# Seven products in all four pairs of every second MLP step of a two-layer decoder trunk, and a new order of the pairs in the other steps

## The chip, the cores and the metric

The kernel runs on one core of one Trainium2 chip. The metric is the device time of one execution in microseconds (us), the median of several runs; before the change it is 2121.18 us over three runs (2120.37 to 2121.22). TensorE (PE) multiplies matrices, VectorE (DVE) and ScalarE (ACT) work elementwise, POOL and SP issue transfers (DMA); PEld in the profile is TensorE's weight load, which overlaps its matmuls.

## The reference, cut to what matters

Two layers on one sequence of 256 tokens, model width 2048. Layer 0 mixes by a short convolution, layer 1 by stick-breaking attention; each is followed by an MLP with 8192 hidden units, and every part is normalised before and after. Only the MLPs are changed:

```python
def sq_relu_mlp(u, w_up, w_down):
    return jnp.square(jax.nn.relu(u @ w_up)) @ w_down

def reference(x, ...):
    ...
    for i in range(DEPTH):
        ...
        h = h + rmsnorm(m, mix_post_g[i])
        u = rmsnorm(h, mlp_pre_g[i])
        h = h + rmsnorm(sq_relu_mlp(u, mlp_w_up[i], mlp_w_down[i]), mlp_post_g[i])
        ...
```

## The kernel before

Everything is float32. For TensorE each operand is cut into a high part, rounded by ScalarE (whi, hi), and a low part, the rest, taken by VectorE (wlo, lo); one product is three matmuls: high by high, high by low, low by high.

**The steps of an MLP.** The 64 tiles of 128 hidden units are made in STEPS = 8 groups of eight. The first group comes from `lead_up`. Then in each of the steps e = 0 to 6 TensorE alternates eight times between two jobs: `whole_up` makes one hidden tile of the next group (16 matmuls of 512 columns with high parts of the weights, 16 of 256 with low parts, into the one bank UP_BANK), and `Down.pair` multiplies two hidden tiles of the present group by their rows of the down weights. A step has two halves, h = 0 and 1. Each half walks the four pairs m = 0 to 3 for one band of 1024 output columns. I call one up tile with its down pair a place; a step has eight. Step 7 has only down pairs.

**Pairs of eight and of seven.** A pair is a 2x2 by 2x2 product of blocks: two halves of the tokens and two hidden tiles on one side, two hidden tiles and two halves of the band's columns on the other. `eight` does it with eight products, 24 matmuls. `seven` does it with seven (a scheme of Strassen's kind), 21 matmuls, for which sums of blocks are needed on both sides. `split_seven` forms four differences of the weights on VectorE (t1 to t4, line 200, into a buffer with one copy, tag gpre) and cuts seven blocks into parts, in four tiles a, b, t, u of 512, 1024, 1024 and 1024 columns; a pair of eight cuts two weight chunks of 1024. `sums_of` (line 891) forms four sums of the hidden blocks. The table SEVEN says which pairs of a step go by seven: m = 1, 2, 3 in both halves of steps 0 to 6, pair 0 alone in step 7. For a pair of eight the hidden side keeps a difference (`dif`) instead.

**What sets the order.** TensorE's order is that of the code. VectorE's and ScalarE's is fixed when the program is built, by a scheduler that takes the code's order, its priorities and the dependencies. Weights come as chunks of 512 KB from SP, in the order of `step_chunks`, into RAW = 5 buffers; a buffer is loaded again once its chunk is cut. The parts lie in a ring of RING = 7 high and 7 low tiles. `finish` frees the up bank: ScalarE copies one half of it (`half`, line 927), VectorE adds the other (`s`, line 861), and the next up tile can begin.

**The end of a down projection.** An object `Down` collects one band over eight pairs: the second half of a step and the first half of the next. At its last pair VectorE adds three banks into the results (line 968), ScalarE copies four others out (line 983), and POOL adds these into the results by transfers (line 931, three with each of the next up tiles). So it always ends with the fourth place of a step, and the fifth follows, a pair of eight here.

Of the kernel before, what the change touches and what calls it, by code (L numbers as in the profile page):

```python
# [9 lines left out]
F32 = mybir.dt.float32  # L10
F32R = mybir.dt.float32r
# [3 lines left out]
P = 128  # L15
# [31 lines left out]
STEPS = 8  # L47
NF = FF // STEPS // P
UP_BANK = 2
DOWN_BANKS = {(0, 0): 3, (0, 1): 4, (1, 0): 5, (1, 1): UP_BANK, 1: 6, 5: 7, 6: 0, 7: 1}  # L50
LAST_BANKS = [[6, 7], [0, 1]]
SEVEN = [((1, 2, 3), (1, 2, 3))] * 7 + [((0,), ())]

IN_N = [j * KD + i for i in range(KD) for j in range(3)]

# [11 lines left out]
def band_of(e, h):  # L67

    return 1 - (h + e) % 2


def step_chunks(e):

    return [
        (kind, c)
        for h in range(2) for m in range(4)
        for kind, c in [("up", 8 * h + 2 * m + t) for t in range(2)]
        + [("dn", band_of(e, h) * 8 + 2 * m + t) for t in range(2)]
    ]

# [6 lines left out]
def trunk(ctx, tc, x, xT, vecs, rows, ws, out):  # L87
# [149 lines left out]
    def operand(name):  # L237
        return act.tile([P, 4, 2, NB, P], F32R, tag="x4", name=name)
# [119 lines left out]
    def inverse_root(total, bias, scale=1.0 / D):  # L358
        r = small("rstd")
        nc.scalar.activation(r[:], total, AF.Sqrt, bias=bias, scale=scale)  # L360
        nc.vector.reciprocal(r[:], r[:])
        return r

    class Norms:
# [119 lines left out]
        def input(self, b, c):  # L484

            self.u[b, c] = piece(h[b], c)
            if self.gpre is not None:
                t = self.u[b, c] = self.pool.tile([P, 6 * P], F32, tag="hg", name="hg", bufs=4)[:, :512]
                with tc.high_priority():
                    nc.vector.tensor_tensor(t, piece(h[b], c), piece(self.gpre, c), op=ALU.mult)  # L490

# [121 lines left out]
    class OutNorms(Norms):  # L613
# [6 lines left out]
            self.order.__enter__()  # L620

        def post(self, b, c, src, to, scale=None):
            t = self.pool.tile([P, 6 * P], F32, tag="hg", name="mgg", bufs=4)[:, :512] if c > 1 else to
            nc.scalar.activation(
                self.dump()[:], src, AF.Square, scale=1.0 if scale is None else scale,
                accum_out=self.ss[b][:, c : c + 1],
            )
            self.gained(b, c, src, t, scale)
            if (b, c) == (1, 2):
                self.residual(0, 3, [0])  # L630
            if c == 2:
                self.add_up(b)
            elif c == 3:
                self.r[b] = inverse_root(self.ss[b][:, 3:4], self.bias[b][:])
                for i in range(3):
# [198 lines left out]
    def mlp(pool, i, before, after):  # L834
# [5 lines left out]
        def two_parts(parts, src):  # L840
            hi, lo = parts
            nc.scalar.activation(hi, src, AF.Copy)
            nc.vector.tensor_tensor(lo, src, hi.bitcast(F32), op=ALU.subtract)

        class Hidden:


            def __init__(self, e):
                self.xs, self.sums = [None] * (NF // 4), {}
                first, second = SEVEN[e]  # L850
                self.pairs = [2 * m for m in first]
# [6 lines left out]
            def tile(self, n, ps, half):  # L858
                s = pool.tile([P, T], F32, tag="s", name="s", bufs=3)
                with tc.high_priority():  # L860
                    nc.vector.tensor_tensor(s[:], ps[:, :T], half[:], op=ALU.add)  # L861
                nc.scalar.activation(s[:], s[:], AF.Relu)  # L862
                nc.scalar.activation(s[:], s[:], AF.Square)
                if self.xs[n // 4] is None:
                    self.xs[n // 4] = operand("hid4")
                if n in self.pairs and n not in self.apart:
                    two_parts(self.x(n, 0), s[:, :P])
                else:
                    split_tile(self.xs, n, s[:])
                if n in self.pairs:  # L870
                    held[n] = s
                elif n - 1 in self.pairs:
                    self.sums[n - 1] = self.sums_of(n - 1, held.pop(n - 1), s)
                elif n - n % 2 in self.eights:
                    if n % 2 == 0:
                        self.sums[n] = pool.tile([P, 2, 2, P], F32R, tag="d", name="sums", bufs=2)
                    parts = [self.sums[n - n % 2][:, n % 2, j, :] for j in range(2)]
                    d = pool.tile([P, P], F32, tag="dif", name="dif", bufs=1)
                    nc.vector.tensor_tensor(d[:], s[:, :P], s[:, P:], op=ALU.subtract)
                    two_parts(parts, d[:])  # L880

            def sums_of(self, n, x, y):

                t = after.dump()
                s1, s2, s3, s4 = (t[:, j * P : (j + 1) * P] for j in range(4))
                a11, a21, a12, a22 = x[:, :P], x[:, P:], y[:, :P], y[:, P:]
                for to, v, w, op in (
                    (s1, a21, a22, ALU.add), (s2, s1, a11, ALU.subtract),
                    (s3, a11, a21, ALU.subtract), (s4, a12, s2, ALU.subtract),
                ):  # L890
                    nc.vector.tensor_tensor(to, v, w, op=op)
                if n in self.apart:
                    one = pool.tile([P, 2 * P], F32R, tag="s1", name="sums", bufs=1)
                    one = [one[:, j * P : (j + 1) * P] for j in range(2)]
                else:
                    one = self.x(n, 1)
                more = pool.tile([P, 6 * P], F32R, tag="hg", name="sums", bufs=4)
                more = [more[:, j * 3 * P : (j + 1) * 3 * P] for j in range(2)]
                two_parts(one, s1)
                two_parts(more, t[:, P:])  # L900
                return [one] + [[m[:, j * P : (j + 1) * P] for m in more] for j in range(3)]
# [99 lines left out]
        class Down:  # L1001


            def __init__(self, j, plan):
                self.j, self.plan, self.ps = j, plan, {}
                sevens_at = [at for at in plan if at[1] in SEVEN[at[0]][at[2]]]
                whole_at = [at for at in plan if at not in sevens_at and at[0] == STEPS - 1]
# [17 lines left out]
            def pair(self, at, first, xs):  # L1025
                e, m, _ = at
                seven = m in SEVEN[e][at[2]]
                (self.seven if seven else self.eight)(at, first, xs, 2 * m)
# [42 lines left out]
        for e in range(STEPS):  # L1071
            for h in range(2):
                for m in SEVEN[e][h]:
                    n = 16 * h + 4 * m + 2 if e < STEPS - 1 else 8 * h + 2 * m
                    sevens[W["mlp", i, e + 1].base + n] = pool
        now = Hidden(0)
        lead_up(now)
        for e in range(STEPS):
            first = W["mlp", i, e + 1].base
            if e == STEPS - 1:  # L1080
                for b in range(NB):
                    scale[b] = small("hs")
                    nc.vector.tensor_tensor(scale[b][:], before.hs[b][:], before.hs[b][:], op=ALU.mult)
                after.gpost = row(pool, (B_MPOST0, B_MPOST1)[i], "gpost")
                turned["banks"] = [2, 3]
                for m in range(4):
                    down.pair((e, m, 0), first + 2 * m, now)
                run(
                    [Group(first + 8, 8, now.xs, LAST_BANKS, lambda b, c, ps: add(band_of(e, 1), b, c, ps, True))],
                    leave=after,  # L1090
                )
                break
            new = Hidden(e + 1)
            for h in range(2):
                if e == 0 or h == 1:
                    plan = [(e, m, h) for m in range(4)]
                    if h == 1:
                        plan += [(e + 1, m, 0) for m in range(4)]
                    down = Down(band_of(e, h), plan)
                for m in range(4):  # L1100
                    at_chunk = first + 16 * h + 4 * m
                    whole_up(new, 4 * h + m, at_chunk, UP_BANK)
                    down.pair((e, m, h), at_chunk + 2, now)
            now = new

# [180 lines left out]
    for j in range(4):  # L1286
        for i, (name, to, scale) in enumerate((
            ("k", kT, lambda b: kv.hs[b][:]), ("q", qT, lambda b: held["rq", b][:]),
        )):
            n = 2 * j + i  # L1290
# [86 lines left out]
```

## Time and profile before

| | |
|---|---|
| median of three runs | 2121.18 us (2120.37 to 2121.22) |
| profiled execution | 2121.52 us, its span 2119.8 us |
| matmuls on TensorE | 10816 |
| VectorE, ScalarE instructions | 2557, 2136 |
| TensorE's granted clock, mean | 0.999 of full |
| DMA packets | 449.24 MB in all, mean 212 GB/s |

The span runs from the first to the last instruction; the profiled execution's own time is 1.7 us longer. The first MLP takes about 380 to 1021 us of the span, the second about 1450 to its end. A row of a timeline has the start (us), the duration (us), engine, line, operation, the tiles written and read, shapes and a count; a bracket tells how long the engine stood idle before and for whom. Durations on TensorE and VectorE overlap a little with the next instruction, so the distance of two starts is the better price of an instruction in a row of many.

### The profile page before, as it was taken

What the parts mean: (1) busy time and instruction counts of PE and PEld (TensorE: products, weight loads), DVE (VectorE), ACT (ScalarE), POOL (GpSimd) and SP (SyncE); (2) the same over time, 40 slices, a digit from 0 to 9 for tenths busy, and PEclk for the clock granted to TensorE, in tenths of its full rate; (3) what the DMA queues carried; (4) which work ended last, traced back from release to release, by engine and by line L of the source; (5) the groups of instructions that cost most, each with busy time, mean ns of one, the idle gap of its engine ahead of it and who ended that gap; (6) DMA issues with size and microseconds to landing.
All of it is one profiled execution on the core that took longest, in us unless ns stands there. A gap on an engine that the chain in (4) does not pass through costs nothing.

```text
span 2119.8 us, 29868 instructions
## 1 busy us (share of the span) xinstructions
PE 2109.0 (99%) x10816; PEld 1805.5 (85%) x10816; DVE 1700.5 (80%) x2557; ACT 1389.6 (66%) x2136; POOL 112.6 (5%) x135
## 2 busy tenths in 40 slices
PE   9999999999999999999999999999999999999998
PEld 8888888888888888888888888889888888888886
DVE  7766655889889888989866777558898889898987
ACT  7554444777766766766567888547767667676664
POOL 0000000010110100101000000000101001011010
PEclk9999999999999999999999999999999999999999
DMA  8655564676877867869575545655678688687693
GB/s 314 214 188 189 189 238 140 206 224 216 253 210 221 249 205 237 243 202 272 163 229 173 159 159 159 218 179 183 201 223 237 209 238 245 203 255 220 210 265 138
DMA packets 132341, 449.24 MB, mean 212 GB/s; under 512 B 14816, under 2 KB 15072, under 8 KB 131168
## 3 DMA queue, kind: packets, MB, share of 16 engines
q1 hardware_dynamic: 113472, 408.65, 58.7%
q0 software_dynamic: 18432, 38.28, 9.2%
q8 instruction: 85, 1.39, 0.3%
q14 instruction: 64, 0.52, 0.1%
q10 hardware_dynamic: 288, 0.39, 0.1%
HBM read 413.19 MB, written 2.10 MB: 196 GB/s over the span
## 4 chain that ended last, share of the span: by engine, by line
PE 99%; DMA 0%; DVE 0%; ACT 0%; SPq 0%; issue 0%; DVEq 0%; ACTq 0%
PE up L914 21%; PE up L921 12%; PE acc L719 11%; PE acc L300 8%; PE acc L302 8%; PE acc L301 7%; PE acc L1021 5%; PE acc L1022 5%; PE acc L1023 5%; PE more L1022 4%; PE more L1021 4%; PE more L1023 4%; PE lead L719 1%; PE up L916 1%; PE tr L253 1%; DMA raw<-w_in 0%
## 5 line engine op out<-in xcount | busy, mean ns | idle before, releaser
L174 DVE TENSOR_TENSOR wlo<-raw,whi 128x1024 fp32r<-128x1024 f32 (+1 forms) x506 | 605.2, 1208 | 201.3 <-ACT whi L163 129.9
L163 ACT ACTIVATE whi<-raw 128x1024 fp32r<-128x1024 f32 (+1 forms) x506 | 525.7, 1046 | 232.3 <-PE acc L302 84.0
L914 PE MATMUL up<-u,whi 128*128 128x512 f32 x1952 | 465.0, 389 | 0.0
L914 PEld LDWEIGHTS up<-u,whi 128*128 128x128 f32 x1952 | 365.0, 188 | 74.7
L921 PEld LDWEIGHTS up<-u,wlo 128*128 128x128 f32 x2048 | 263.6, 191 | 10.3
L921 PE MATMUL up<-u,wlo 128*128 128x256 f32 x2048 | 268.0, 283 | 0.0
L931 POOL DMA_DIRECT2D mg<-more x108 | 100.3, 977 | 1292.1 <-ACT s L862 582.7
L176 DVE SCALAR_TENSOR_TENSOR wlo<-raw,gv,whi 128x512 fp32r<-128x512 f32 (+1 forms) x160 | 131.8, 853 | 41.5 <-ACT whi L163 40.8
L719 PE MATMUL acc<-u,whi 128*128 128x512 f32 x672 | 156.5, 390 | 0.0
L300 PE MATMUL acc<-whi,u 128*128 128x512 f32 x384 | 153.1, 399 | 0.1
L163 ACT ACTIVATE whi<-raw,gv 128x512 fp32r<-128x512 f32 (+1 forms) x160 | 121.6, 800 | 48.2 <-PE acc L302 42.0
L302 PE MATMUL acc<-whi,u 128*128 128x512 f32 x384 | 149.9, 390 | 0.0
L301 PE MATMUL acc<-wlo,u 128*128 128x512 f32 x384 | 149.7, 390 | 0.0
L719 PEld LDWEIGHTS acc<-u,whi 128*128 128x128 f32 x672 | 124.8, 188 | 25.0
L927 ACT ACTIVATE half<-up 128x256 f32<-128x256 f32 x128 | 48.7, 383 | 113.6 <-PE up L921 112.0
L200 DVE TENSOR_TENSOR sums<-raw,sums 128x512 f32<-128x512 f32 x172 | 117.8, 685 | 1.5
L302 PEld LDWEIGHTS acc<-whi,u 128*128 128x128 f32 x384 | 72.1, 188 | 15.3
L719 PEld LDWEIGHTS acc<-u,wlo 128*128 128x128 f32 x672 | 83.5, 192 | 1.7
L719 PE MATMUL acc<-u,wlo 128*128 128x256 f32 x672 | 84.2, 283 | 0.0
L300 PEld LDWEIGHTS acc<-whi,u 128*128 128x128 f32 x384 | 72.2, 188 | 13.9 <-ACT tk L1214 0.6
L301 PEld LDWEIGHTS acc<-wlo,u 128*128 128x128 f32 x384 | 72.3, 188 | 13.4
L862 ACT ACTIVATE s<-s 128x256 f32<-128x256 f32 x128 | 52.1, 410 | 33.5 <-DVE s L861 32.4
(4476 smaller groups left out, 4065.5 us busy)
## 6 DMA issues: line engine op xcount, KB each, us to landing
raw<-w_mlp SPq DMA_DIRECT2D x512, 512.0 KB, 4.7
raw<-w_in SPq DMA_DIRECT2D x94, 512.0 KB, 4.2
mg<-more POOLq DMA_DIRECT2D x108, 256.0 KB, 8.0
raw<-w_out SPq DMA_DIRECT2D x32, 512.0 KB, 3.6
raw<-w_v SPq DMA_DIRECT2D x32, 512.0 KB, 4.4
raw<-w_k SPq DMA_DIRECT2D x32, 512.0 KB, 4.0
raw<-w_q SPq DMA_DIRECT2D x32, 512.0 KB, 3.7
raw<-w_wo SPq DMA_DIRECT2D x32, 512.0 KB, 3.7
```

The lines of the kernel that those rows point to most:

```text
L163: rounded = nc.scalar.activation(hi[:, at], raw[i][:, at], AF.Copy, scale=1.0 if gain is None else gain)
L174: nc.vector.tensor_tensor(lo[:, at], t[:, at], hi[:, at].bitcast(F32), op=ALU.subtract)
L176: nc.vector.scalar_tensor_tensor(lo[:, at], t[:, at], gain, hi[:, at].bitcast(F32), op0=ALU.mult, op1=ALU.subtract)
L300: nc.tensor.matmul(ps[:], xh, hi[:, a], start=i == 0 and k == 0, stop=False)
L301: nc.tensor.matmul(ps[:], xh, lo[:, a], start=False, stop=False)
L302: nc.tensor.matmul(ps[:], xl, hi[:, a], start=False, stop=i == self.n - 1 and k == self.ks - 1)
L719: nc.tensor.matmul(ps[:, :cols], w, xs[:, :cols], start=k == 0 and part == parts[0], stop=k == KD - 1 and part == parts[1], skip_group_che ...
L914: nc.tensor.matmul(ps, weight(0, first, m), x, start=k == 0, stop=False)
L921: nc.tensor.matmul(pss[n][:, :T], weight(1, first, m), x, start=False, stop=k == KD - 1)
L1021: nc.tensor.matmul(self.ps[key][:], xh, hi, start=first, stop=False)
L1022: nc.tensor.matmul(self.ps[key][:], xh, lo, start=False, stop=False)
L1023: nc.tensor.matmul(self.ps[key][:], xl, hi, start=False, stop=last)
```

## The change

In steps 0, 2, 4 and 6 all four pairs go by seven products in both halves. In steps 1, 3 and 5 pair 0 still goes by eight; the first half walks the pairs 0, 1, 2, 3 as before, the second 1, 2, 3, 0, so that the pair of eight stands first and last in the step. The second half of every step uses that order, in the stored weights too. Step 7 is as it was. The buffers of the sums become one of a larger form (tag d, which now also serves `one` in step 7), and the tag hg has five copies in place of four.

```diff
-SEVEN = [((1, 2, 3), (1, 2, 3))] * 7 + [((0,), ())]
+SEVEN = [((0, 1, 2, 3),) * 2 if e % 2 == 0 else ((1, 2, 3),) * 2 for e in range(STEPS - 1)] + [((0,), ())]
+ORDER = ((0, 1, 2, 3), (1, 2, 3, 0))
...
-        for h in range(2) for m in range(4)
-        for kind, c in [("up", 8 * h + 2 * m + t) for t in range(2)]
+        for h in range(2) for i, m in enumerate(ORDER[h])
+        for kind, c in [("up", 8 * h + 2 * i + t) for t in range(2)]
         + [("dn", band_of(e, h) * 8 + 2 * m + t) for t in range(2)]
...
-                t = self.u[b, c] = self.pool.tile([P, 6 * P], F32, tag="hg", name="hg", bufs=4)[:, :512]
+                t = self.u[b, c] = self.pool.tile([P, 6 * P], F32, tag="hg", name="hg", bufs=5)[:, :512]
...
-                        self.sums[n] = pool.tile([P, 2, 2, P], F32R, tag="d", name="sums", bufs=2)
+                        self.sums[n] = pool.tile([P, 2, 2, P], F32R, tag="d", name="sums", bufs=1)
...
-                    one = pool.tile([P, 2 * P], F32R, tag="s1", name="sums", bufs=1)
-                    one = [one[:, j * P : (j + 1) * P] for j in range(2)]
+                    one = pool.tile([P, 2, 2, P], F32R, tag="d", name="sums", bufs=1)
+                    one = [one[:, 0, j, :] for j in range(2)]
...
-                more = pool.tile([P, 6 * P], F32R, tag="hg", name="sums", bufs=4)
+                more = pool.tile([P, 6 * P], F32R, tag="hg", name="sums", bufs=5)
...
-                    n = 16 * h + 4 * m + 2 if e < STEPS - 1 else 8 * h + 2 * m
+                    n = 16 * h + 4 * ORDER[h].index(m) + 2 if e < STEPS - 1 else 8 * h + 2 * m
...
-                    plan = [(e, m, h) for m in range(4)]
+                    plan = [(e, m, h) for m in ORDER[h]]
                     if h == 1:
-                        plan += [(e + 1, m, 0) for m in range(4)]
+                        plan += [(e + 1, m, 0) for m in ORDER[0]]
                     down = Down(band_of(e, h), plan)
-                for m in range(4):
-                    at_chunk = first + 16 * h + 4 * m
-                    whole_up(new, 4 * h + m, at_chunk, UP_BANK)
+                for n, m in enumerate(ORDER[h]):
+                    at_chunk = first + 16 * h + 4 * n
+                    whole_up(new, 4 * h + n, at_chunk, UP_BANK)
                     down.pair((e, m, h), at_chunk + 2, now)
```

How the instructions move is shown at the fifth place of step 4 of the first MLP, just behind the end of a down projection. A line number in the changed kernel is one higher. First TensorE, before: the last half of a pair of eight, each factor of it an ordinary weight chunk (a product is here two times three matmuls, one for each chunk).

```order
L1021 MATMUL acc<-whi_7790,sums 128x512
L1022 MATMUL acc<-wlo_7791,sums 128x512
L1023 MATMUL acc<-whi_7790,sums 128x512
L1021 MATMUL acc<-whi_7826,sums 128x512
L1022 MATMUL acc<-wlo_7827,sums 128x512
L1023 MATMUL acc<-whi_7826,sums 128x512
L1021 MATMUL more<-whi_7790,hid_6631 128x512
L1022 MATMUL more<-wlo_7791,hid_6631 128x512
L1023 MATMUL more<-whi_7790,hid_6631 128x512
L1021 MATMUL more<-whi_7826,hid_6631 128x512
L1022 MATMUL more<-wlo_7827,hid_6631 128x512
L1023 MATMUL more<-whi_7826,hid_6631 128x512
```

After: the last part of the pair of seven in its place, with t and u, the differences of the weights (290 is the pair's first chunk).

```order
L1022 MATMUL more<-whi290t,hid_6673 128x512
L1023 MATMUL more<-wlo290t,hid_6673 128x512
L1024 MATMUL more<-whi290t,hid_6673 128x512
L1022 MATMUL more<-whi290t,sums 128x512
L1023 MATMUL more<-wlo290t,sums 128x512
L1024 MATMUL more<-whi290t,sums 128x512
L1022 MATMUL more<-whi290u,sums 128x512
L1023 MATMUL more<-wlo290u,sums 128x512
L1024 MATMUL more<-whi290u,sums 128x512
L1022 MATMUL acc<-whi290u,hid_6673 128x512
L1023 MATMUL acc<-wlo290u,hid_6673 128x512
L1024 MATMUL acc<-whi290u,hid_6673 128x512
```

The pair has 21 matmuls now in place of 24, three for each of seven products. Next VectorE at the same place, before: the low part of the pair's first chunk, then s of the fourth place's up tile, two of the three additions of the finished down projection (line 968), the pair's second chunk, the chunks of the next up tile (wlo_7833, wlo_7847) and work on hidden sums (sq, hid).

```order
L174 TENSOR_TENSOR wlo_7791<-raw_7702,whi_7790 128x1024
L861 TENSOR_TENSOR s<-up,half 128x256
L968 TENSOR_TENSOR mg<-mg,acc 128x512 x2
L174 TENSOR_TENSOR wlo_7827<-raw_7704,whi_7826 128x1024
L891 TENSOR_TENSOR sq<-s 128x128
L174 TENSOR_TENSOR wlo_7833<-raw_7732,whi_7832 128x1024
L968 TENSOR_TENSOR mg<-mg,acc 128x512
L248 TENSOR_TENSOR hid_7468<-s,hid_7468 128x256
L891 TENSOR_TENSOR sq<-sq,s 128x128
L843 TENSOR_TENSOR hid_7468<-sq,hid_7468 128x128
L891 TENSOR_TENSOR sq<-s,sq 128x128
L174 TENSOR_TENSOR wlo_7847<-raw_7746,whi_7846 128x1024
```

After: s stands behind the low parts of the fifth up tile's second chunk and of the pair's a; the parts b and t of the pair lie between the additions (line 969 now).

```order
L175 TENSOR_TENSOR wlo_7796<-raw_7700,whi_7795 128x1024
L175 TENSOR_TENSOR wlo290a<-raw_7755,whi290a 128x512
L862 TENSOR_TENSOR s<-up,half 128x256
L969 TENSOR_TENSOR mg<-mg,acc 128x512
L175 TENSOR_TENSOR wlo290b<-raw_7757,whi290b 128x1024
L969 TENSOR_TENSOR mg<-mg,acc 128x512
L892 TENSOR_TENSOR sq<-s 128x128
L175 TENSOR_TENSOR wlo290t<-sums,whi290t 128x1024
L969 TENSOR_TENSOR mg<-mg,acc 128x512
L249 TENSOR_TENSOR hid_7524<-s,hid_7524 128x256
L892 TENSOR_TENSOR sq<-sq,s 128x128
L844 TENSOR_TENSOR hid_7524<-sq,hid_7524 128x128
```

Ahead of s VectorE now has the four differences of the fifth pair, and behind it the low parts of b, t and u, with u after the rows shown; before, two chunks of 1024 were all of that pair's work.

More of the change, by code (lines that the diff above doesn't have):

```diff
@@ L622, in post @@
         def post(self, b, c, src, to, scale=None):
-            t = self.pool.tile([P, 6 * P], F32, tag="hg", name="mgg", bufs=4)[:, :512] if c > 1 else to
+            t = self.pool.tile([P, 6 * P], F32, tag="hg", name="mgg", bufs=5)[:, :512] if c > 1 else to
             nc.scalar.activation(
```

## The prediction

> **What bounds the kernel now.** I read the page first, then TensorE's waits, then windows of one MLP step.
>
> ```profile
> span 2119.8 us, 29868 instructions
> PE 2109.0 (99%) x10816; PEld 1805.5 (85%) x10816; DVE 1700.5 (80%) x2557; ACT 1389.6 (66%) x2136; POOL 112.6 (5%) x135
> ...
> PE 99%; DMA 0%; DVE 0%; ACT 0%; SPq 0%; issue 0%; DVEq 0%; ACTq 0%
> ```
>
> ```profile
> PE warm L709 <- DVE ones L104: 1.1, 1, 1.1
> PE lead L719 <- ACT whi L163: 0.7, 1, 0.7
> PE tr L253 <- DVE h L480: 0.3, 1, 0.3
> ```
>
> The chain is TensorE alone, and these are all the waits it has (us, times, longest): 2.1 us. VectorE's 80% is an average over stages, so I take the MLP apart. The next rows are windows (length, then busy time of PE, PEld, DVE, ACT, POOL, the granted clock, DMA share, GB/s): eight pairs of an MLP, then one pair of eight products and one of seven, each from the first matmul of its up tile to that of the next.
>
> ```profile
> 787.00:871.00 84.00, 84.00 (x431) 72.05 (x431) 74.70 (x111) 57.91 (x89) 7.94 (x10) 1.00 0.77 229
> ```
>
> ```profile
> 788.64:799.65 11.01, 11.01 (x57) 9.43 (x56) 10.06 (x18) 6.85 (x14) 4.42 (x5) 1.00 1.05 265
> 799.65:809.98 10.33, 10.33 (x55) 8.86 (x53) 9.54 (x13) 7.51 (x11) 2.61 (x3) 1.00 1.08 284
> ...
> 851.96:862.29 10.33, 10.33 (x54) 8.86 (x53) 10.05 (x16) 7.33 (x12) 0.00 (x0) 1.00 0.69 213
> ```
>
> TensorE has no hole at the full clock. A pair of eight takes 11.01 us, one of seven 10.33; two of eight and six of seven make 2 x 11.01 + 6 x 10.33 = 84.0 us, the window. VectorE works 74.7 of these 84.0 us: it is second, 9.3 us behind, and what the change gives it to do decides the case.
>
> **What is removed.** The order of TensorE has 48 matmuls of 128x512 less: in steps 0, 2, 4 and 6 of both MLPs two pairs go from eight products in 24 matmuls to seven in 21, so 4 x 2 x 2 = 16 pairs by 3. Their pace, from rows whose first matmuls start 16 apart:
>
> ```profile
> 851.96 3.79 PE L914 MATMUL up<-u,whi 128*128 128x512 f32 x16
> 855.59 2.08 PE L921 MATMUL up<-u,wlo 128*128 128x256 f32 x16
> ```
>
> (855.59 - 851.96) / 16 = 0.227 us, so 48 x 0.227 = **10.9 us**; the two kinds of pair say the same, 16 x (11.01 - 10.33) = 10.9. Their weight loads go with them. SP issues as many loads as before, since the new place of pair 0 in the second half is changed in the stored weights and in the stream alike, and POOL as many additions. The Trainium skill (TensorE: Matmul & The Clock Gate, section Back-to-back issue gap) gives about 131 ns per matmul of 512 columns in a sustained stream; by that the term would be 6.3 us and the profiled execution 2115.2. This case's trace disagrees, with 227 ns over every such stretch, and the measurement stands.
>
> **What is added.** Each of the 16 pairs now costs VectorE four differences of weights (t1 to t4), and low parts for 3584 columns (a of 512, b, t, u of 1024) in place of 2048.
>
> ```profile
> 802.54 0.68 DVE L200 TENSOR_TENSOR sums<-raw 128x512 f32<-128x512 f32 x1
> 803.14 0.68 DVE L200 TENSOR_TENSOR sums<-raw,raw 128x512 f32<-128x512 f32 x1
> ...
> 862.23 1.23 DVE L174 TENSOR_TENSOR wlo318u<-sums,whi318u 128x1024 fp32r<-128x1024 f32 x1
> 863.37 0.28 DVE L843 TENSOR_TENSOR hid<-s,hid 128x128 fp32r<-128x128 f32 x1
> ```
>
> Back to back a 512-wide operation takes 0.60 us (803.14 - 802.54), a 1024-wide one 1.14 (863.37 - 862.23). So 4 x 0.60 + 1.14 + 0.60 = 4.14 us more per pair, 8.3 us per step of all sevens. ScalarE's high parts grow likewise by a 1024-wide and a 512-wide one:
>
> ```profile
> L163 ACT ACTIVATE whi<-raw 128x1024 fp32r<-128x1024 f32 x498 | 523.0, 1057 | 230.9 <-PE acc L302 84.0 <-PE up L914 67.6 <-PE acc L719 38.3
> L163 ACT ACTIVATE whi<-raw,gv 128x512 fp32r<-128x512 f32 x128 | 85.4, 714 | 35.4 <-PE acc L302 34.0 <-issue 1.4
> ```
>
> about 1.06 + 0.71 = 1.8 us a pair, 57.9 + 3.5 = 61.4 us of a step of 82.6: hidden under TensorE with 21 us to spare; without that cover it would cost 8 x 3.5 = 28. The sums of the hidden tiles change little: where an eight's pair becomes a seven's, two differences of 128x128 with their splits and a 128x256 split give way to four 128x128 sums, a 128x384 and two 128x128 and one 128x256 split, which at the same rows' pace is 0.5 us, and falls in the step before, an odd one with room. The merged sums buffer and the fifth hg buffer add no instruction; a tile of the next step is made after the last product that reads the old one, so I cost them at nothing, covered by TensorE (about 1 us of wait a step, at most 14, if a release came late).
>
> **Does VectorE fit?** A step of all sevens takes TensorE 84.0 - 2 x 0.68 = 82.6 us and VectorE 74.7 + 8.3 = 83.0: 0.4 over. An odd step takes 84.0 and 75.2. So in half the steps VectorE is full, and its waits decide. In the quoted window they are:
>
> ```profile
> DVE wlo310u L174 <- ACT whi310u L208: 2.5, 1, 2.5
> DVE wlo L174 <- PE up L921: 2.3, 1, 2.3
> DVE wlo L174 <- issue: 2.0, 1, 2.0
> DVE wlo294u L174 <- ACT whi294u L208: 1.6, 1, 1.6
> ```
>
> ```profile
> ACT whi294u L208 <- PE more L1023: 2.4, 1, 2.4
> ...
> ACT whi310u L208 <- PE more L1023: 1.8, 1, 1.8
> ```
>
> The two on ScalarE go back to TensorE: the ring of seven parts was full, VectorE was as far ahead as it may be. Such waits vanish once it is late; they are slack, not demand. How late may it be? Two deadlines: the up bank (one bank, freed by s, then taken by the next up tile), and the last parts of the weights.
>
> ```profile
> 815.72 0.38 ACT L927 ACTIVATE half<-up 128x256 f32<-128x256 f32 x1 [1.28 <-PE up L921]
> 816.58 0.42 DVE L861 TENSOR_TENSOR s<-up,half 128x256 f32<-128x256 f32 x1
> 820.30 3.79 PE L914 MATMUL up<-u,whi 128*128 128x512 f32 x16
> ...
> 871.26 0.39 PE L1021 MATMUL more<-whi318u,sums 128*128 128x512 f32 x1
> ```
>
> s ends at 817.00 and the bank is wanted at 820.30: 3.3 us. wlo318u ends at 863.46 and is used from 871.26: 7.8 us. In the run of sevens s follows half at once (0.5 us), so the lag is not growing there today. With 0.4 us too much per step and 3.3 us to hold it until the next pair of eight gives back 4.1, VectorE should just fit. The order keeps s ahead of the next pair's b, t and u parts; behind it wait, in the fifth pair, the three additions of the finished down projection, which a pair of eight used to cover.
>
> A second full place is the first pair of each MLP, right behind the lead-up, which becomes one of seven:
>
> ```profile
> 409.00:451.00 42.00, 42.00 (x224) 36.31 (x224) 39.05 (x71) 31.92 (x61) 0.00 (x0) 1.00 0.54 173
> ```
>
> 39.05 + 4.14 + 0.5 = 43.7 us of VectorE in 42.0 - 0.7 = 41.3: 2.4 over, held for a time by the same two deadlines.
>
> For all this TensorE's stall has no row of before. Below it is nothing (all of the lag held by the bank; it can't be a gain, since TensorE has no wait to lose). Above, if all 9.3 us of idle time stayed, a step would take 83.0 + 9.3 = 92.3 in place of 82.6, 78 us over the 8 steps. Nearest to it are the excesses that the rows give: 8 x 0.4 for the full steps and 2 x 2.4 for the lead-ups, 8.0 us. Each of them alone is under the 3.3 us of the bank and could vanish; I take a fifth for the places where two meet, **1.5 us**.
>
> **Sum.** 2121.52 (the profiled execution: span 2119.8 and 1.7 around it) - 10.9 + 1.5 = 2112.1. The median of the runs, 2121.18, is 0.3 lower, so **2111.8 us**, 9.4 or 0.44% faster. Below about 0.2% (4.2 us) a measurement of this kernel tells nothing.
>
> **Rival 1, VectorE takes over (slower).** Its order is fixed, and in a full step each wait that isn't TensorE's doing comes back as a hole of TensorE. For it: 83.0 against 82.6, and the runs of up to nine sevens in a row where there were three. Against: the waits above are TensorE's. It decides when more than about 1.0 us a step (a step then exceeds 84.0) is lost for good. With half of the idle time kept, a step takes 83.0 + 4.65 = 87.7, 3.7 over 84.0: 8 x 3.7 = 29 us over today, **2151**.
>
> **Rival 2, the loads pace it (no change).** When a down projection ends, POOL's additions into the results crowd the queues:
>
> ```profile
> raw<-w_mlp SPq DMA_DIRECT2D x512, 512.0 KB, 4.7
> ```
>
> ```profile
> L147 SPq DMA_DIRECT2D raw<-w_mlp x9: 327/328/328, 788.2 to 808.4; - x9
> ...
> DMA to landing us min/median/max: 5.4/7.4/8.4
> ```
>
> ```profile
> DVE sums L200 <- DMA raw<-w_mlp: 3.7, 4, 1.7
> ```
>
> The first row is the median over all loads (4.7 us), the next that stretch (7.4), the last VectorE's waits at 451 to 475, where such additions begin in step 0. A seven holds both raw buffers until its differences are done, so loads start late when time is short. For it: the DMA share of 1.05 and 1.08 in the pairs above, now under a seven too. Against: at 787 to 871 VectorE waits for no load. If each of the 14 ends cost 3.7 us, less the 3.3 of the bank but with the 0.5 by which s lags already, 14 x 0.9 = 12.6 us would be lost: 2121.2 - 10.9 + 12.6 = **2122.9**.
>
> **Rival 3, it doesn't do what it says.** The saved matmuls could be missing, at 2121.2. The order shows them gone and nothing else new on TensorE.
>
> **Chances.** The forecast 0.66; rival 1 0.16; rival 2 0.16; rival 3 0.02. The forecast's case runs from no stall, 2121.2 - 10.9 = 2110.3, to four times the stall, 2116. Rival 2 scatters to both sides of 2121, a quarter of it still below 2116.9. The range **2109.5 to 2124** holds the forecast, most of rival 2 and rival 3; its low end is no stall less the 0.8 between the runs. Rival 1 is left out but for its foot, since the price between nothing and 78 us has no upper row near. Faster by over 0.2%: 0.66 + 0.04 = 0.70; within: 0.10; slower: 0.20.
>
> **What would show it.** Eight pairs of an even step in 82.6 us with PE busy throughout and no row of TensorE waiting for s or for wlo; VectorE near 82 of these, its ring waits gone; odd steps at 84.0. Wrong it is if TensorE waits for s (the bank) or wlo in the fifth to eighth pair of even steps (rival 1), or VectorE's t1 and t3 wait for raw with holes of TensorE right behind, at the ends of the down projections (rival 2).

## The result, and the profile after

| | before | after |
|---|---|---|
| median, the same chip (us) | 2121.2 (2120.37 to 2121.41) | 2112.5 (2111.68 to 2113.6) |
| ratio, 95% interval | | 0.996 (0.9947 to 0.9973) |
| profiled execution, its span (us) | 2121.52, 2119.8 | 2111.68, 2110.0 |

The change makes the kernel 8.7 us faster; forecast were 9.4 us and 2111.8. The profiled execution is the fastest of the six runs after the change, so its profile may show less of what is lost than a median run would.

First the page of the changed kernel: its head, the busy time of each engine (us, share, instructions), and the chain of work that ended last.

```profile
span 2110.0 us, 29980 instructions
...
PE 2098.2 (99%) x10768; PEld 1795.9 (85%) x10768; DVE 1766.0 (84%) x2669; ACT 1409.4 (67%) x2168; POOL 112.6 (5%) x135
...
PE 96%; DVE 1%; DMA 1%; ACT 0%; issue 0%; SPq 0%; DVEq 0%; ACTq 0%
```

TensorE has 48 matmuls less and its busy time fell by 2109.0 - 2098.2 = 10.8 us. Its idle time grew from 2119.8 - 2109.0 = 10.8 to 2110.0 - 2098.2 = 11.8 us. The chain, which was TensorE alone, now leaves it for VectorE and a transfer for 1% each. VectorE's busy time grew by 65.5 us and ScalarE's by 19.8; POOL's is the same.

TensorE's waits in the changed kernel (us in total, times, longest) name the place where the chain leaves it:

```profile
PE up L915 <- DVE s L862: 1.3, 2, 0.8
PE warm L710 <- DVE ones L105: 1.1, 1, 1.1
PE lead L720 <- ACT whi L164: 0.4, 2, 0.2
```

The first row is new: twice an up tile waits for s, which frees its bank. To find where, here are windows of the first MLP, one per step from 0 to 4 (length, then busy time of PE, PEld, DVE, ACT, POOL, the granted clock, DMA share, GB/s):

```profile
409.84:492.50 82.66, 82.66 (x426) 70.93 (x425) 80.19 (x125) 63.03 (x105) 7.05 (x8) 1.00 0.72 212
492.50:576.50 84.00, 83.16 (x427) 71.02 (x426) 76.45 (x114) 58.72 (x93) 7.01 (x8) 1.00 0.77 236
...
577.61:660.20 82.59, 82.59 (x425) 70.90 (x424) 79.86 (x117) 61.07 (x93) 7.91 (x9) 1.00 0.75 224
660.20:744.20 84.00, 84.00 (x431) 72.02 (x430) 78.70 (x122) 58.26 (x92) 7.92 (x9) 1.00 0.76 240
744.20:826.80 82.60, 82.60 (x425) 70.90 (x424) 79.63 (x112) 60.83 (x91) 7.92 (x9) 1.00 0.73 221
```

Every even step takes 82.6 us with TensorE busy throughout. Only the window of step 1 has a hole (83.16 of 84.00 busy; the window is one of 84 us laid over the step, so it doesn't hold all of a step that has grown). Inside step 1, the fifth, sixth and seventh place in the same columns:

```profile
534.49:544.82 10.33, 10.33 (x54) 8.86 (x53) 10.30 (x18) 10.33 (x19) 5.27 (x6) 1.00 0.90 182
544.82:556.15 11.33, 10.49 (x55) 8.68 (x53) 7.26 (x11) 4.58 (x8) 1.74 (x2) 1.00 1.06 300
555.83:566.30 10.47, 10.15 (x52) 8.73 (x53) 10.47 (x17) 7.94 (x13) 0.00 (x0) 1.00 0.70 231
```

All three are places with a pair of seven and should take 10.33 us. The sixth takes 11.33 and the seventh 10.47. In the second MLP the same two places of step 1 take 10.91 and 10.47. Together 1.00 + 0.14 + 0.58 + 0.14 = 1.9 us are lost there, and no other place of a step is longer than its 10.33 or 11.01. In the sixth place VectorE is busy for only 7.26 of 11.33 us: it isn't short of time there, it waits. Its timeline in the first MLP (start, duration, operation, and in brackets how long it stood idle before and for whom):

```profile
549.94 0.69 DVE L201 TENSOR_TENSOR sums<-raw 128x512 f32<-128x512 f32 x1 [1.37 <-DMA raw<-w_mlp]
553.33 0.69 DVE L201 TENSOR_TENSOR sums<-raw,raw 128x512 f32<-128x512 f32 x1 [2.70 <-DMA raw<-w_mlp]
553.94 1.22 DVE L175 TENSOR_TENSOR wlo<-raw,whi 128x1024 fp32r<-128x1024 f32 x1
555.07 0.69 DVE L201 TENSOR_TENSOR sums<-raw,sums 128x512 f32<-128x512 f32 x1
555.68 0.42 DVE L862 TENSOR_TENSOR s<-up,half 128x256 f32<-128x256 f32 x1
```

and on ScalarE and TensorE what s belongs to:

```profile
550.56 0.38 ACT L928 ACTIVATE half<-up 128x256 f32<-128x256 f32 x1
```

```profile
548.45 2.08 PE L922 MATMUL up<-u,wlo 128*128 128x256 f32 x16
...
556.15 3.93 PE L915 MATMUL up<-u,whi 128*128 128x512 f32 x16 [0.84 <-DVE s L862]
```

ScalarE's half is done at 550.94, and s could start. VectorE starts it at 555.68, because its fixed order has three differences and a low part ahead of s, and two of the differences wait for chunks that haven't landed (1.37 and 2.70 us). s ends at 556.10, and TensorE's next up tile starts at 556.15, 0.84 us after the engine ran dry. The loads behind it, by SP's queue from 535 to 557, with the time from issue to landing:

```profile
L148 SPq DMA_DIRECT2D raw<-w_mlp x6: 327/328/1351, 541.6 to 555.2; - x6
...
DMA to landing us min/median/max: 4.8/8.3/11.5
```

In that window the first load is issued at 541.6, and a load takes 8.3 us at the median and up to 11.5, against 4.7 over all loads of the kernel before. Two things meet at 535 to 545. First, a buffer comes free late. ScalarE is busy for all 10.33 us of the fifth place, VectorE for 10.30. ScalarE copies results of the finished down projection (L984) beside its usual work, and the high parts for the sixth up tile stand behind the copies; VectorE takes the first low part after that, and the load follows its end:

```profile
537.88 1.09 ACT L984 ACTIVATE more<-more 128x512 f32<-128x512 f32 x2
538.83 2.04 ACT L164 ACTIVATE whi<-raw 128x1024 fp32r<-128x1024 f32 x2
```

```profile
540.34 1.22 DVE L175 TENSOR_TENSOR wlo<-raw,whi 128x1024 fp32r<-128x1024 f32 x1
```

Second, POOL's additions run (5.27 and 1.74 us of POOL in the two places) while the late loads are under way. That is a reading of the rows; the experiments test it.

The fourteen ends of down projections in the steps 0 to 6 (seven in each MLP) differ in how long VectorE waits for loads behind them. In windows of some 25 us it waits 4.1 us behind the end above, and behind that of step 1 in the second MLP (from 1602 to 1628)

```profile
DVE sums L201 <- DMA raw<-w_mlp: 3.7, 2, 2.2
```

These are the two ends that lose, and both waits are longer than the 3.3 us that the prediction read as the up bank's room. Behind the other twelve VectorE waits 0 to 2.6 us, and TensorE loses nothing.

### The profile page after: what moved, and what is told of

Same layout as the page of the kernel before. It is cut to its first block, busy times and chain, and to the rows that moved or that the text cites. A ratio compares the mean times of both kernels' runs of the same rounds, so it can differ in the third digit from the quotient of the medians.

```text
span 2110.0 us, 29980 instructions
## 1 busy us (share of the span) xinstructions
PE 2098.2 (99%) x10768; PEld 1795.9 (85%) x10768; DVE 1766.0 (84%) x2669; ACT 1409.4 (67%) x2168; POOL 112.6 (5%) x135
## 4 chain that ended last, share of the span: by engine, by line
PE 96%; DVE 1%; DMA 1%; ACT 0%; issue 0%; SPq 0%; DVEq 0%; ACTq 0%
PE up L915 20%; PE up L922 11%; PE acc L720 11%; PE acc L301 8%; PE acc L303 8%; PE acc L302 8%; PE more L1023 5%; PE more L1022 5%; PE more L1024 5%; PE acc L1022 4%; PE acc L1023 4%; PE acc L1024 4%; PE lead L720 1%; PE up L917 1%; DMA raw<-w_mlp 1%; PE tr L254 1%
## 5 line engine op out<-in xcount | busy, mean ns | idle before, releaser
L175 DVE TENSOR_TENSOR wlo<-raw,whi 128x1024 fp32r<-128x1024 f32 (+1 forms) x474 | 566.5, 1206 | 149.4 <-ACT whi L164 123.7
L164 ACT ACTIVATE whi<-raw 128x1024 fp32r<-128x1024 f32 (+1 forms) x474 | 489.7, 1045 | 206.5 <-PE acc L303 84.0
L201 DVE TENSOR_TENSOR sums<-raw,sums 128x512 f32<-128x512 f32 x204 | 139.5, 684 | 1.3
```

The costliest lines, as they stand in the source:

```text
L164: rounded = nc.scalar.activation(hi[:, at], raw[i][:, at], AF.Copy, scale=1.0 if gain is None else gain)
L175: nc.vector.tensor_tensor(lo[:, at], t[:, at], hi[:, at].bitcast(F32), op=ALU.subtract)
L201: nc.vector.tensor_tensor(t, x, y, op=ALU.subtract)
```

## The experiments

The kernel before took 2121.0 to 2121.2 us on the chips of these runs. Each time is a median with its range, each ratio is to the kernel before.

**1. The old order of pairs.** The even steps keep their sevens; in the second half of a step the pairs go 0, 1, 2, 3 again, so the fifth place of an odd step is a pair of eight.

```diff
-ORDER = ((0, 1, 2, 3), (1, 2, 3, 0))
+ORDER = ((0, 1, 2, 3), (0, 1, 2, 3))
```

> The changed kernel with the order 0, 1, 2, 3 in both halves, as before the change: in odd steps the pair of eight stands first and fifth again. My theory: the whole 10.9 us come from the 48 matmuls, and what is lost (2.2 us of the median) is lost where a load comes late behind the end of a down projection in step 1, with a pair of seven in the fifth place. With the pair of eight back there the loss of step 1 goes: 2110.3 to 2111.3, and TensorE doesn't wait for s in step 1. Rival (the new order is what lets the sevens fit): VectorE falls behind without it, 2114 or more, with TensorE waiting for s or for wlo in several steps.

Measured: 2110.18 us (2110.07 to 2111.34), ratio 0.9951 (0.9938 to 0.9963); none of its runs is as slow as the fastest of the change. No row of TensorE waiting for s is left. The sixth place of step 1 in windows, and SP's loads from 535 to 557:

```profile
545.40:555.73 10.33, 10.33 (x54) 8.86 (x53) 7.78 (x10) 5.99 (x9) 0.98 (x2) 1.00 1.02 279
```

```profile
L148 SPq DMA_DIRECT2D raw<-w_mlp x8: 328/328/1244, 539.7 to 556.2; - x8
...
DMA to landing us min/median/max: 3.7/7.2/10.7
```

The place is whole again, and the time is the expected one to 0.1 us. The loads still land late (7.2 us), but the first is issued 1.9 us earlier. It follows the low part of the sixth up tile's first chunk, as in the change; VectorE starts that part at 538.40 here and at 540.34 there, ScalarE the high part ahead of it at 536.97 and at 538.83. With a pair of eight in the fifth place both engines have less to do ahead of it. So with the old order the sevens of the even steps gain 10.8 us, and the new order gives 2.3 of it back. (The profile has small losses yet: the seventh and eighth places of step 0 are up to 0.2 us longer than they should be.)

**2. The new order alone.** SEVEN as before the change; order and buffers as in the change.

```diff
-SEVEN = [((0, 1, 2, 3),) * 2 if e % 2 == 0 else ((1, 2, 3),) * 2 for e in range(STEPS - 1)] + [((0,), ())]
+SEVEN = [((1, 2, 3),) * 2 for e in range(STEPS - 1)] + [((0,), ())]
```

> The new order alone: pair 0 goes by eight products in all steps 0 to 6 as before the change, but stands last in each second half. My theory: no matmul goes, so nothing is won, and the fifth place is now a seven behind each end of a down projection: 2121.2 to 2122.5, with at most a stall for s in step 1. Rival (part of the gain is the order's): under 2119.

Measured: 2124.28 us (2123.07 to 2125.4), ratio 1.0015 (1.0006 to 1.0024): 3.3 us slower than before, more than expected. TensorE's waits of this kernel:

```profile
PE up L915 <- DVE s L862: 1.4, 4, 0.4
```

The holes lie in the sixth and seventh places of steps 0 and 1 in both MLPs, with a little in step 2 of the first. The same wait appears with no added product of seven anywhere, behind the same ends, where a pair of seven now stands in the fifth place.

The order is not all that is new here, though. The diff leaves one copy of the buffer for an eight's sums (tag d) where there were two, and of the same form. The changed kernel has pairs of eight in every second step only, and one copy is enough. Here every step has them, and the old sums are read until the eighth place. So the second difference (`dif`) of the first two hidden tiles that step 0 makes, done at 432.04 in the kernel before, is done at 497.74 in this one:

```profile
432.04 0.28 DVE L879 TENSOR_TENSOR dif<-s 128x128 f32<-128x128 f32 x1
```

```profile
497.74 0.28 DVE L880 TENSOR_TENSOR dif<-s 128x128 f32<-128x128 f32 x1
```

One of the three copies of s is held all that time. Steps 3 to 6 hold it as long and have no hole, so this alone makes none; but how much of the 3.3 us is the order's and how much the buffer's isn't shown. The clean price of the order is that of experiment 1.

**3. s ahead of the differences.** The differences t1 to t4 are issued on VectorE only after the latest s, so that s can't stand behind a load.

```diff
-                    nc.vector.tensor_tensor(s[:], ps[:, :T], half[:], op=ALU.add)
+                    latest.append(nc.vector.tensor_tensor(s[:], ps[:, :T], half[:], op=ALU.add))
...
-            nc.vector.tensor_tensor(t, x, y, op=ALU.subtract)
+            if latest:
+                with tc.issue_after(latest[-1].ins):
+                    nc.vector.tensor_tensor(t, x, y, op=ALU.subtract)
```

> The changed kernel with one rule more for VectorE's order: the four differences of a pair's weights are issued after the s of the up tile ahead, so that s is not queued behind a wait for a load. My theory: the differences can wait (7.8 us of room) and s cannot (3.3), so the stall for s goes: 2110.3 to 2111.3. Rival (VectorE is simply too full): it then waits for s with work behind it, the weights' low parts come late and TensorE waits for wlo instead: 2113 or more.

Measured: 2113.01 us (2112.1 to 2114.46), ratio 0.9963 (0.995 to 0.9975), no gain over the change. Its waits on TensorE:

```profile
PE more L1028 <- DVE wlo554a L176: 0.8, 1, 0.8
PE acc L1028 <- DVE wlo170b L176: 0.8, 1, 0.8
PE acc L1028 <- DVE wlo554b L176: 0.8, 1, 0.8
```

The wait for s is gone, and TensorE waits for low parts of weights in place of it, now in step 0 (its seventh place takes 12.23 and 12.47 us in the two MLPs). The differences that were held back are what is late next. This is what the rival said, in its time and its wait, and my theory missed: the differences had no such room. Moving s cures the symptom only.

**4. No additions by POOL.** The additions of four banks into the results are left out, and with them that part of the output's sum; all else stays.

```diff
-                with tc.issue_after(copied.ins):
-                    nc.gpsimd.dma_start(a, more, accum_op=ALU.add)
+                pass
```

> The changed kernel without POOL's additions into the results at the ends of the down projections (that part of the sum is left out). If the late loads are the cause of what is lost, as I think, they are in time again and TensorE has no wait for s: 2110.3 to 2110.9. Rival (VectorE's own load is the cause): the stall stays, 2111.7 to 2112.5.

Measured: 2110.32 us (2109.77 to 2110.99), ratio 0.995 (0.9937 to 0.9962). No place of a step has a hole. SP's loads from 535 to 557 again:

```profile
L148 SPq DMA_DIRECT2D raw<-w_mlp x8: 327/328/328, 542.0 to 555.4; - x8
...
DMA to landing us min/median/max: 3.6/4.8/6.8
```

The first load is issued as late as in the change (542.0 against 541.6), so the additions aren't what makes its issue late. But loads land in 4.8 us in place of 8.3. VectorE's waits for them from 535 to 560, in the changed kernel

```profile
DVE sums L201 <- DMA raw<-w_mlp: 4.1, 2, 2.7
```

and without the additions

```profile
DVE sums L201 <- DMA raw<-w_mlp: 0.5, 1, 0.5
```

fall from 4.1 us to 0.5, and the stall is gone. The additions in the loads' way are therefore necessary for it, as expected.

**5. The first results copied by VectorE.** Where the first banks of a band go into the results, VectorE copies them in place of ScalarE.

```diff
-                    nc.scalar.activation(r, ps[:], AF.Copy)
+                    nc.vector.tensor_copy(r, ps[:])
```

> The changed kernel with the first three results of each band (ends of the down projections in steps 0 and 1, until now copied by ScalarE) copied by VectorE. My theory: what sets step 1 apart from the later steps, where nothing is lost, is that ScalarE copies eight banks there in place of five, so that high parts, and with them the release of the raw buffers, come late just when POOL's additions crowd the queues. With five copies the stall in step 1 goes: 2110.3 to 2111.3. Rival (the additions crowd the loads whoever copies): as the changed kernel, 2111.7 to 2113.6, or more, as VectorE has 1.8 us more to do there.

Measured: 2112.66 us (2111.73 to 2113.54), ratio 0.996 (0.9948 to 0.9973), as the change. Its waits on TensorE:

```profile
PE more L1023 <- DVE wlo554a L175: 0.7, 1, 0.7
PE up L915 <- DVE s L862: 0.4, 1, 0.4
```

The holes of step 1 are gone, others came: step 0's seventh place takes 11.35 and 11.83 us in the two MLPs, and the sixth and seventh behind one end, in step 6 of the second MLP, 10.92 and 10.46. The time is the rival's, and my theory of the copies missed. SP's loads from 541 to 557 show what the copies did to them:

```profile
L148 SPq DMA_DIRECT2D raw<-w_mlp x7: 327/328/465, 541.6 to 556.0; - x7
...
DMA to landing us min/median/max: 5.6/7.6/8.5
```

The first is issued at 541.6 as in the change: with three copies fewer on ScalarE it comes no earlier. What spares step 1 is VectorE's order, which came out another way. A low part now stands between the two differences that waited in the change, only the second still waits (0.98 us), and s follows that one at once:

```profile
551.49 1.21 DVE L175 TENSOR_TENSOR wlo<-raw,whi 128x1024 fp32r<-128x1024 f32 x1
553.68 0.69 DVE L201 TENSOR_TENSOR sums<-raw,raw 128x512 f32<-128x512 f32 x1 [0.98 <-DMA raw<-w_mlp]
554.29 0.42 DVE L862 TENSOR_TENSOR s<-up,half 128x256 f32<-128x256 f32 x1
```

The load for the second difference is no earlier (it starts at 553.68, in the change at 553.33), yet s starts at 554.29 in place of 555.68. Unloading ScalarE onto a VectorE this full moves the loss and doesn't remove it.

**6. How much room VectorE has.** In every pair of seven part of t1 is formed twice, with the same result: all 512 columns in the first two runs (0.60 us by the prediction's row), 128 in the third (0.20 us, estimated from the 0.28 us row of a 128-wide operation and the overlap of such rows).

```diff
+            if t is t1:
+                nc.vector.tensor_tensor(t[:, :512], x[:, :512], y[:, :512], op=ALU.subtract)
```

In the kernel before, all 512 columns:

> The kernel before with the same second t1: 3.6 us more of VectorE in each step, 78.3 of 84.0. My theory: hidden by the 9.3 us of idle time, 2121.2 to 2122. Rival (VectorE's idle time is no slack): 2125 or more.

In the changed kernel, all 512 columns:

> The changed kernel with t1 formed twice, 0.60 us more for VectorE in each pair of seven: 4.8 us in a step of all sevens, 3.6 in an odd step. If VectorE is as full as the prediction's sum says (83.0 of 82.6 us), such a step asks 87.8 and TensorE loses about 5 us in each of 8 steps less what the bank holds: 2125 to 2150, with waits for s or wlo in every even step. Rival (there is room yet, the loss is only the late loads of step 1): 2112 to 2117.

In the changed kernel, 128 columns:

> The changed kernel with a quarter of t1 formed twice, 0.20 us more for VectorE in each pair of seven, 1.6 us in a step of all sevens. VectorE was busy 80 of such a step's 82.6 us, so 81.6 still fit: 2112.5 to 2114. Rival (it is full to the brim and every 1.6 us shows): 8 steps by 1.6, 2119 or more.

| kernel | added per step of 6 or 8 sevens (us) | median (us) | against its own base (2121.2, 2112.5) |
|---|---|---|---|
| before, 512 columns | 3.6 | 2121.13 (2120.76 to 2122.01) | ratio 1.0001 (0.9992 to 1.001) |
| change, 512 columns | 3.6 or 4.8 | 2128.93 (2128.58 to 2131.45) | 16.4 us more; to before 1.004 (1.0027 to 1.0053) |
| change, 128 columns | 1.2 or 1.6 | 2113.25 (2111.05 to 2115.85) | 0.8 us more; to before 0.9965 (0.9952 to 0.9977) |

TensorE's waits with 512 columns in the changed kernel, the first rows:

```profile
PE acc L1025 <- DVE wlo L175: 2.6, 2, 1.3
PE up L917 <- DVE s L864: 1.5, 5, 0.6
PE acc L1025 <- DVE wlo234b L175: 1.2, 1, 1.2
```

Before the change 3.6 us a step disappear in VectorE's idle time. After it about 1.4 us a step still nearly do, and 4 us don't: 16.4 us come through of the 61 us added (2771 - 2669 = 102 more instructions of VectorE by 0.60), with holes in the steps 0 to 5 of both MLPs, for low parts of weights and for s. This is rival 1's world, and by the medians the changed kernel stands between 1.4 and 4 us a step from it. The lower end is loose: the five runs with 128 columns scatter from 2111.05 to 2115.85, and the profiled one, at 2115.41, has places of up to 12.43 us in step 6 of the first MLP and of 11.51 in step 0 of the second. All three times came out as expected (the first to 0.1 us), but the theory of 2125 to 2150 wanted holes in every even step, and step 6 has none of size.

**7. Fewer pairs of eight, in the old order.** Three kernels: no step with pairs of eight in steps 0 to 6; pairs of eight in step 1 alone; in steps 1 and 6.

```diff
-SEVEN = [((0, 1, 2, 3),) * 2 if e % 2 == 0 else ((1, 2, 3),) * 2 for e in range(STEPS - 1)] + [((0,), ())]
-ORDER = ((0, 1, 2, 3), (1, 2, 3, 0))
+SEVEN = [((0, 1, 2, 3),) * 2 if e != 1 else ((1, 2, 3),) * 2 for e in range(STEPS - 1)] + [((0,), ())]
+ORDER = ((0, 1, 2, 3), (0, 1, 2, 3))
```

None (the condition dropped):

> All four pairs by seven in all of the steps 0 to 6, with the order 0, 1, 2, 3 in both halves: 12 more pairs lose 3 matmuls each, 8.2 us. No pair of eight is left where VectorE can catch up. If a step asks 83.0 of 82.6 us of VectorE, the 14 steps lose 0.4 each and about 1 each behind the additions: 2110 to 2125. If VectorE's true demand is that of back-to-back starts (81.6), 2102 to 2106.

Step 1 alone (the diff above):

> Order 0, 1, 2, 3 in both halves; pairs of eight only in step 1, where the changed kernel loses its time, all others of steps 0 to 6 by seven: 24 pairs fewer matmuls than before the change, 16.3 us off 2121.2, 2104.9 without any stall. My theory: step 1 is covered again, what remains are the stalls that the run without any pair of eight shows in steps 0, 3 or 4 and 6, 0.5 to 1.7 each: 2106 to 2109. Rival (the stalls come from VectorE having no step to recover in): more than is saved over the run without a pair of eight, 2104.5 to 2106.

Steps 1 and 6 (the condition e not in (1, 6)):

> As the run with pairs of eight only in step 1, with step 6 having them too: 20 pairs fewer matmuls, 13.6 us off 2121.2, 2107.6 without any stall. My theory: the two steps with the largest stalls are covered, 2107.6 to 2108.6, so no better than no pair of eight at all. Rival (most of what is lost sits in other steps): 2109 to 2111.

Without a stall each added pair of seven takes 0.68 us off 2121.2.

| pairs of eight in | pairs changed | without a stall | measured median (us) | ratio |
|---|---|---|---|---|
| no step | 28 | 2102.1 | 2107.96 (2106.28 to 2110.79) | 0.9939 (0.9927 to 0.9952) |
| step 1 | 24 | 2104.9 | 2105.67 (2104.68 to 2107.31) | 0.9929 (0.9917 to 0.9942) |
| steps 1 and 6 | 20 | 2107.6 | 2107.97 (2107.17 to 2108.5) | 0.9938 (0.9925 to 0.9952) |
| steps 1, 3, 5 (experiment 1) | 16 | 2110.3 | 2110.18 (2110.07 to 2111.34) | 0.9951 (0.9938 to 0.9963) |

Two windows of the kernel without pairs of eight, about a step each, and its first row of TensorE's waits:

```profile
576.00:659.00 83.00, 83.00 (x427) 71.20 (x426) 82.09 (x124) 59.32 (x93) 7.91 (x9) 1.00 0.80 232
741.00:824.00 83.00, 83.00 (x427) 71.23 (x427) 82.97 (x126) 59.95 (x94) 7.91 (x9) 1.00 0.78 233
```

```profile
PE up L915 <- DVE s L862: 6.6, 6, 2.1
```

In the second window VectorE has no idle time left (82.97 of 83.00), and TensorE has none in either. Against the sum without a stall the median loses 5.9 us; in the profiled run, the slowest of the five, nearly all that is lost lies in the sixth and seventh places of six steps, right behind the ends of down projections (12.62 us the longest). The median lies between the two ranges that I had named (2102 to 2106 and 2110 to 2125), so neither reading of VectorE's demand came out. With pairs of eight in step 1 alone the median is 0.8 us above the sum without a stall and the kernel the fastest of all: 15.5 us under the one before, 6.8 under the change. Its wait for s:

```profile
PE up L915 <- DVE s L862: 0.3, 1, 0.3
```

I had expected 2106 to 2109 for it; the rival's 2104.5 to 2106 holds the time, which fits that one step in which VectorE catches up is nearly enough. The kernel with steps 1 and 6 came within its 2107.6 to 2108.6.

## Why the prediction was right, step by step

**What bounds the kernel.** Right. TensorE's busy time fell by 10.8 us and the profiled time by 9.84, which is that less 1.0 of new idle time.

**The 10.9 us of removed matmuls.** Right to 0.2: where nothing stalls the median falls by 2121.0 - 2110.18 = 10.8 us (experiment 1) or 10.7 (experiment 4), and the even steps take the 82.6 us that were forecast. That is 10.7 / 48 = 0.223 us or more for each matmul. The other price that the prediction weighed, 131 ns for a matmul (the Trainium skill, TensorE: Matmul & The Clock Gate, section Back-to-back issue gap), would have given 6.3 us. The runs disagree, with their 10.7 us or more.

**The work added to VectorE and ScalarE.** 16 x 4.14 + 8 x 0.5 = 70 us were forecast for VectorE, and 65.5 came; 16 x 1.8 = 28 for ScalarE, and 19.8 came. Over the whole stretch of an MLP the extra work of ScalarE is hidden, as said. Not so at one place: in step 1's fifth place ScalarE is busy for all of 10.33 us, and a mean with 21 us to spare didn't show that.

**Does VectorE fit.** The outcome is right: no hole in any even step of the profiled run. The balance step by step is not. It put 83.0 us of work into an even step and 75.2 into an odd one; the rows show 79.6 to 80.2 and 76.5 to 78.7. Step 5, behind the last of the windows above, is

```profile
826.80:910.70 83.90, 83.90 (x431) 71.97 (x430) 78.35 (x121) 57.94 (x91) 7.91 (x9) 1.00 0.76 240
```

so an even and an odd step together hold 79.63 + 78.35 = 158.0 us, against the 158.2 forecast. So the sum was right and its cut at the step's border wrong: VectorE does part of an even step's work in its neighbours. For this reason the "0.4 over" of a full step and the "2.4 over" behind the lead-up show no hole in the changed kernel. They were not far from one, though: experiments 3 and 5 opened one in step 0, at its seventh place.

**The stall of 1.5 us.** The size is near by luck: the mechanism behind it was another. 10.9 - 8.7 = 2.2 us are missing from the gain on medians, 1.9 in the places of the profiled run. I took a fifth of the excesses of full steps and lead-ups, a share for which there was no row, and none of it was found there. What occurs is the mechanism of rival 2, which I had as a case of its own: at the end of a down projection the loads land late, t1 and t3 hold up VectorE's fixed order, and s stands behind them. Its price for an end was right too (0.9 us; measured 1.14 and 0.72), but not how often it is paid: at 2 of the 14 ends, not all of them. So the sign that the prediction named for rival 2 did show, t1 and t3 waiting for loads with a hole of TensorE right behind, and the forecast's own sign, no row of TensorE waiting for s, did not. Experiment 4 shows that the additions cause the late landing, and experiment 1 that the order of the pairs makes it count.

**The order of the pairs.** The prediction spoke of the fifth place only in that a pair of eight "used to cover" the additions behind it, and gave the new order no price. That is the term that is missing: 2.3 us in the changed kernel (2112.5 - 2110.18, experiment 1). The single sums buffer and the fifth hg copy, put at nothing, cost nothing that shows there: experiment 1 has them and loses 0.1 us by the medians. With pairs of eight in every step (experiment 2) the single buffer does hold work up.

**The deadlines.** The 3.3 us of the bank decide where the prediction said they would: s came 0.5 us behind half in the quoted row, with 3.3 us left, and could be 3.8 late; here it starts 555.68 - 550.94 = 4.7 us behind half, 0.9 too much, and TensorE stands still for 0.84. The 7.8 us of the low parts were read at one place and don't hold everywhere: in experiment 3 step 0 has no such room (its seventh place is 1.9 and 2.1 us too long).

**Rival 1** did not occur, but experiment 6 puts it within 4 us of VectorE a step. The kernel without pairs of eight comes near to it, with VectorE at 82.97 of 83.00 us; but what it loses lies behind the ends of down projections, so late loads and too much work aren't told apart there.

**What stays open.** Why the loss falls into step 1 and no other. Late landing behind the additions is needed for it, and the order of VectorE decides which end pays. That ScalarE's copies are part of it isn't shown: experiment 5 took three away, and the first late load was issued no earlier. For step 0 in experiments 3 and 5 the additions and VectorE's lateness weren't told apart. More buffers for the chunks, which might uncouple the loads, weren't tried.

## What to carry to other kernels

When work is given to the second engine, look for the place where a transfer, a copy and the new work meet, and not only at its sum over a step: the sum here was right to 0.2 us, and the loss came from one place in which VectorE was idle for a third of the time. An instruction that frees a bank for the bounding engine should not stand, in a fixed order, behind one that waits for a load; but moving it helps only if what it is moved ahead of has room of its own. Put the cheaper step for the crowded engine right behind the crowd, and try how few such steps suffice: one in seven did here, to within 0.8 us.

## What the runs showed of the hardware

POOL's adding transfers slow the weight loads more than their bytes suggest. The same kernel's loads in the same stretch took 4.8 us at the median and 6.8 at most without them, 8.3 and 11.5 with them. In the changed kernel from 533 to 557 the queues show (packets, MB, share of 16 engines' time; the first is the additions' queue, the second that of the loads):

```profile
q0 software_dynamic: 1145, 2.09, 54.0%
q1 hardware_dynamic: 1076, 3.90, 43.4%
```

The additions moved about half as many bytes as the loads and took more of the DMA engines' time, 2.3 times as much for each MB.

VectorE at 82.97 busy of 83.00 us still kept TensorE without a hole in that window. A second engine that is full need not stall the first in the same stretch.
